# Weight sums of the first two Strassen chunks: GpSimd additions in SBUF instead of queue transfers and VectorE sums

## The chip, the cores and the metric

The kernel runs on one core of one Trainium2 chip. The metric is the device time of one launch in microseconds (us): lower is better, and the median of several runs counts. Five engines work side by side, each through its own list of instructions in order: TensorE (PE in the profile, with its weight loads shown apart as PEld), VectorE (DVE), ScalarE (ACT), GpSimd (POOL) and SyncE (SP). SP issues most transfers. POOL also has a transfer queue of its own, and only transfers of that queue are used here to add to what already lies in SBUF. About 0.2% of the time, 1.9 us, is what a measurement of this kernel can tell from no change.

## The reference: what is computed

The reference is a two-layer encoder trunk over 512 tokens of width 1024, in float32, with 256 memory tokens. Cut to its skeleton:

```
for i in range(2):
    h = rmsnorm(x, norm_g[i]);  mem_h = rmsnorm(mem, mem_norm_g[i])
    proj = h @ w_in                       # q, k, v of the mixer, q_mem, gate
    o_mix = mixer_dilated(...) if i == 0 else mixer_axial_gqa(...)
    o_mem = memory_attention(q_mem, mem_h, w_mem_kv[i], ...)
    y = concat(o_mix, o_mem) * silu(gate)
    x = x + y @ w_out[i]
```

Nearly all of the arithmetic is in the products with the weights `w_in`, `w_mem_kv` and `w_out`. Layer 0 has three groups of q, k and v of eight heads each, so its input projection is by far the widest. The value projection of the first group (columns 6144 to 7167 of `w_in_a`) and the memory queries (columns 9216 to 9727) are the two products that this change touches.

## The kernel before, in words

**Precision.** A float32 operand is split in a rounded high part and the low remainder, and a product is three matmuls: high by high (L178), low activation by high weight (L179), high activation by low weight (L182). For a weight tile of 128 by 1024 the high part `wh` is a cast by ScalarE (L333) and the low part `wo` is a subtraction by VectorE, `wo = wl - wh` (L347), with both inputs in SBUF. The first two chunks, the keys and values of the memory, have a variant with a gain (L331 and L345) and no Strassen sums.

**Strassen chunks.** All further weight products go in chunks (`s_chunk`), each by a Strassen-Winograd scheme of seven products. A chunk has four weight quarters, 11, 12, 21 and 22, and needs three more tiles that are sums of them, and the fourth of them in a quarter's place: T1 = 12 + 11, T2 = 22 + T1, T3 = 12 + 22, T4 = 21 + T2. The seven products take the weights in the order 21, 11, T1, T2, 22, T3, T4 (`ORDER`, L190). The activations' side has its own sums, made by VectorE from the transposed, normalized tokens: S1 and S3 straight from the transposes (L659, L660), S2 and S4 from those (L683, L685), each split in two parts by ScalarE and VectorE (L166 and L169, L671 and L674).

**The order of the chunks.** `PLAN` lists the chunks and `SEQ` their order: the memory keys and values (plan positions 1 and 2), then position 0, the value projection of the first head group, which is the first Strassen chunk, then position 3, the memory queries, which is the second, then the heads. In the code `c` is the plan position. Position 0 has two tiles to each quarter (below 21 of half 0 and of half 1, T1 of half 0, and so on); each of its fourteen steps is twelve matmuls of 128 by 512. Position 3 has one tile to a quarter, and seven steps.

**How the sums were made.** `Weights.dma` issues the loads from SP as far ahead as a limit on live tiles allows: for T1 the quarter 12 is loaded, for T2 the quarter 22. Then `Weights.sum`, called once per step, picks the first sum that is due:

- T1: VectorE adds tile 11 to it in SBUF (L291).
- T2: a transfer of POOL's queue adds tile T1 to it, SBUF to SBUF (L296).
- T3: a transfer of POOL's queue adds quarter 22 from memory (L301, issued in L260).
- T4: a transfer of POOL's queue adds tile T2 to tile 21, which is done with by then (L306).

"Due" is counted in steps, not in time: `self.g` counts steps, and a sum is due so many steps after its inputs were issued. For position 0 the first T1 is held until step 7 and the first T3 until step 10 (`SUM_AT`). So the place of a sum in its engine's list is fixed when the program is built, and the engine runs it when its semaphores allow. `hi` and `lo` (L319, L338) then make `wh` and `wo`, at most four tiles ahead of the matmuls (`RING`).

Of the kernel before, what the change touches and what calls it, by code (L numbers as in the profile page):

```python
# [13 lines left out]
ALU = mybir.AluOpType  # L14
# [27 lines left out]
SEQ = [1, 2, 0] + list(range(3, len(PLAN)))  # L42
T4_AT = {4: 4}
T1_DMA = 15
SUM_AT = {"T1": 7, "T3": 10}
KEEP_C = {0: 14, 3: 14, 4: 12}
KEEP = {"T2": 8, "T2b": 6, "W3": 10, "W1": 9, "W2": 10, "W2s": 9, "W1bs": 9, "W2c": 9, "W1b": 7, "W2b": 9, "W1o": 7}
# [86 lines left out]
def trunk_kernel(ctx: ExitStack, tc: tile.TileContext, x, mem, wall, norm_g, mem_norm_g, gcol,  # L134
                 qn_a, kn_a, qn_b, kn_b, ident_d, mask_d, tab_a, tab_b, out):
    nc = tc.nc
    V, A, G, T = nc.vector, nc.scalar, nc.gpsimd, nc.tensor
# [62 lines left out]
    class Weights:  # L200
        def __init__(self):
            self.items, self.last, self.need, self.allocs, self.sums = [], [], [], [], []
            self.users, self.kinds = {}, []
            g = 0
            for c in SEQ:
                kind, d = PLAN[c], sum(pieces(k) for k in PLAN[:c])
                base = len(self.items)
                if kind in GROUPS:
# [10 lines left out]
                else:  # L219
# [10 lines left out]
                    for k in order:  # L230
                        for x in range(n):
# [5 lines left out]
                            if k != "T4":  # L237
                                self.users[c, k, x] = 1 if k in ("22", "T3") or k == "11" and c >= T1_DMA else 2
                            g += 1
                self.kinds += [kind] * (g - len(self.kinds))  # L240
            assert sum(pieces(k) for k in PLAN) == wall.shape[0]
            self.g = -1
            self.live = 0
# [18 lines left out]
        def dma(self, most=9):  # L262
            while self.allocs and self.live < KEEP_C.get(self.allocs[0][0][0], KEEP[self.allocs[0][2]]) and most:
# [6 lines left out]
                    self.at[key] = self.g  # L270
                self.load(nc.sync, self.tile[key], d)

        def ripe(self, at, key, force, n=None):
            return key in at and (force or self.g - at[key] >= (LEAD if n is None else n))

        def sum(self, force=False, want=None):

            for n, (key, d) in enumerate(self.sums[:8]):
                if want and key != want:
                    continue  # L280
                c, k, x = key
                if not c and not force and self.g < SUM_AT.get(k, 0):
                    break
                if k == "T1" and c >= T1_DMA:
                    if not self.ripe(self.load_at, key, force):
                        continue
                    self.load(G, self.tile[key], d, accum_op=ALU.add)
                elif k == "T1":
                    if not (self.ripe(self.load_at, key, force, 4 if c in KEEP_C else None) and self.ripe(self.at, (c, "11", x), force)):
                        continue  # L290
                    V.tensor_tensor(self.tile[key], self.tile[key], self.tile[c, "11", x], ALU.add)  # L291
                    self.use((c, "11", x))
                elif k == "T2":
                    if not (self.ripe(self.load_at, key, force) and self.ripe(self.at, (c, "T1", x), force, 1 if c < T1_DMA else None)):
                        continue
                    G.dma_start(self.tile[key], self.tile[c, "T1", x], accum_op=ALU.add)  # L296
                    self.use((c, "T1", x))
                elif k == "T3":
                    if not self.ripe(self.load_at, key, force):
                        continue  # L300
                    self.load(G, self.tile[key], d, accum_op=ALU.add)  # L301
                else:
                    if not (self.ripe(self.lo_at, (c, "21", x), force, 1) and self.ripe(self.at, (c, "T2", x), force, T4_AT.get(c))):
                        continue
                    self.tile[key] = self.tile[c, "21", x]
                    G.dma_start(self.tile[key], self.tile[c, "T2", x], accum_op=ALU.add)  # L306
                    self.use((c, "T2", x))
                self.at[key] = self.g
                self.sums.pop(n)
                return True  # L310
            return False
# [7 lines left out]
        def hi(self, force=False):  # L319
            i = self.n_hi  # L320
            if i >= len(self.items) or not self.ripe(self.at, self.items[i], force, 1 if self.items[i][1] == "T1" and self.items[i][0] < T1_DMA else None):
                return False
# [1667 lines left out]
```

## Time and profile before

| | us |
|---|---|
| median of 3 runs (range) | 933.12 (932.94 to 933.17) |
| the profiled execution, its own time | 933.17 |
| its span, first to last instruction | 931.4 |
| TensorE busy | 924.8 |
| VectorE busy | 801.7 |
| ScalarE busy | 695.7 |
| GpSimd busy | 360.5 |

The profile is one execution on the chip. A row of the timeline gives the start in us from the span's start, the duration in us, the engine, the line of the kernel, the operation, the tile that it writes and those that it reads, the shape, and how many instructions are merged in the row (x2); in brackets stands the idle time of the engine just before it and what ended it. Spans of neighbours on one engine overlap a little, because each is reported with its start-up and its drain. A row with the engine PEld is a weight load of TensorE, which runs ahead of the matmul that uses it.

### The profile page before, as it was taken

The page shows a single profiled execution, that of the slowest core. Times are in us where ns is not written, and L with a number is a line of the kernel's source. Part 1 is how long each engine was busy: PE and PEld are TensorE (multiplying, and loading weights), DVE is VectorE, ACT ScalarE, POOL GpSimd, SP SyncE. Part 2 cuts the span into 40 slices and gives each one's busy share as a digit, 9 for nine tenths or more (in the row PEclk, how much of TensorE's full clock was granted, in tenths as well). Part 3 has the DMA queues.
Part 4 walks back from the last instruction along what each step waited for, and adds up shares of the span by engine and source line. Part 5 has one row for each costly group of instructions (what it writes and reads, how often), then busy time and mean ns, then how long its engine had stood idle before and what let it go on. Part 6 is the DMA issues. An engine that isn't in the chain of part 4 may idle for free.

```text
span 931.4 us, 16276 instructions
## 1 busy us (share of the span) xinstructions
PE 924.8 (99%) x5471; PEld 814.7 (87%) x5471; DVE 801.7 (86%) x1457; ACT 695.7 (75%) x1725; POOL 360.5 (39%) x504
## 2 busy tenths in 40 slices
PE   9999999999999999999999999999999999999998
PEld 7789888888888888888889998888988999999886
DVE  6999677879888888979798989999898998789977
ACT  7775789677868686867776767757879887789774
POOL 4411425556564646464746102234252440110122
PEclk9999999999999999999999999999999999999999
DMA  9999948968686778686867899999985687785777
GB/s 351 389 264 331 300 127 218 319 146 247 162 248 166 249 160 271 159 272 135 241 178 207 231 261 271 289 320 331 289 219 114 178 233 178 201 227 116 200 162 181
DMA packets 83179, 212.85 MB, mean 229 GB/s; under 512 B 18960, under 2 KB 25752, under 8 KB 83096
## 3 DMA queue, kind: packets, MB, share of 16 engines
q1 hardware_dynamic: 60744, 141.16, 42.3%
q0 software_dynamic: 20384, 67.12, 39.1%
q10 hardware_dynamic: 1968, 3.54, 1.0%
q8 instruction: 43, 0.70, 0.3%
q14 instruction: 40, 0.33, 0.1%
HBM read 162.96 MB, written 12.65 MB: 189 GB/s over the span
## 4 chain that ended last, share of the span: by engine, by line
PE 91%; DVE 5%; DMA 2%; ACT 1%; SPq 0%; issue 0%; DVEq 0%; ACTq 0%
PE pj L178 24%; PE pj L179 24%; PE pj L182 24%; PE qT L716 3%; PE sa L1476 2%; PE oo L1585 2%; PE ptb L1819 1%; PE sa L1472 1%; DVE wo L347 1%; PE pt L1564 1%; DMA x<-in_x_dram 1%; DMA row<-in_norm_g_dram 1%; PE ob L178 1%; PE ob L182 1%; PE ob L179 1%; PE xT L589 1%
## 5 line engine op out<-in xcount | busy, mean ns | idle before, releaser
L347 DVE TENSOR_TENSOR wo<-wl,wh 128x1024 fp32r<-128x1024 f32 x253 | 308.8, 1225 | 5.6 <-ACT wh L333 5.6
L333 ACT CAST wh<-wl 128x1024 fp32r<-128x1024 f32 x253 | 267.3, 1061 | 27.5 <-PE pj L179 19.5
L178 PE MATMUL pj<-wh,hS 128*128 128x512 f32 (+1 forms) x416 | 154.5, 380 | 0.0
L179 PE MATMUL pj<-wh,hS 128*128 128x512 f32 (+1 forms) x416 | 148.9, 367 | 0.0
L178 PE MATMUL pj<-wh,h 128*128 128x512 f32 (+1 forms) x312 | 115.3, 378 | 0.0
L179 PE MATMUL pj<-wh,h 128*128 128x512 f32 (+1 forms) x312 | 111.6, 367 | 0.0
L536 POOL TENSOR_TENSOR rstd<-mse,half 128x4 f32<-128x4 f32 (+2 forms) x98 | 102.0, 1041 | 8.2
L182 PE MATMUL pj<-wo,hS 128*128 128x512 f32 (+1 forms) x416 | 99.5, 366 | 0.0
L179 PEld LDWEIGHTS pj<-wh,hS 128*128 128x128 f32 x416 | 78.7, 189 | 11.2
L178 PEld LDWEIGHTS pj<-wh,hS 128*128 128x128 f32 x416 | 78.6, 189 | 11.0
L535 POOL TENSOR_SCALAR mse<-hss 128x4 f32<-128x4 f32 (+1 forms) x88 | 45.6, 519 | 104.4 <-ACT junk L704 91.3
L182 PEld LDWEIGHTS pj<-wo,hS 128*128 128x128 f32 x416 | 72.4, 189 | 13.0 <-DVE wo L347 0.2
L704 ACT ACTIVATE junk<-sn 128x128 f32<-128x128 f32 x264 | 79.3, 310 | 3.4 <-DVE sn L428 3.4
L260 POOL DMA_DIRECT2D wl<-in_wall_dram x44 | 41.9, 982 | 95.4 <-DMA wl<-in_wall_dram 21.7
L1417 POOL TENSOR_TENSOR ta<-sn,tabs 128x128 f32<-128x128 f32 (+1 forms) x64 | 38.3, 605 | 104.0 <-DVE sn L709 80.4
L415 ACT COPY sn<-pj 128x512 f32<-128x512 f32 x122 | 67.2, 590 | 12.3 <-PE pj L182 12.3
L182 PE MATMUL pj<-wo,h 128*128 128x512 f32 (+1 forms) x312 | 74.5, 366 | 0.0
L306 POOL DMA_DIRECT2D wl<-wl x35 | 31.0, 895 | 109.2 <-DVE wo L347 48.7
L438 DVE TENSOR_TENSOR sn<-pj,sn 128x512 f32<-128x512 f32 x89 | 60.7, 683 | 6.5 <-PE pj L182 6.2
L179 PEld LDWEIGHTS pj<-wh,h 128*128 128x128 f32 x312 | 59.0, 189 | 8.4
L178 PEld LDWEIGHTS pj<-wh,h 128*128 128x128 f32 x312 | 59.0, 189 | 8.2
L296 POOL DMA_DIRECT2D wl<-wl x35 | 32.9, 964 | 78.7 <-DVE wl L291 18.9
(299 smaller groups left out, 2403.0 us busy)
## 6 DMA issues: line engine op xcount, KB each, us to landing
wl<-in_wall_dram SPq DMA_DIRECT2D x226, 512.0 KB, 7.4
wl<-wl POOLq DMA_DIRECT2D x70, 512.0 KB, 5.9
wl<-in_wall_dram POOLq DMA_DIRECT2D x48, 512.0 KB, 8.6
od<-o SPq DMA_DIRECT2D x9, 256.0 KB, 5.8
x<-in_x_dram SPq DMA_DIRECT2D x4, 512.0 KB
v0r<-sn SPq DMA_DIRECT2D x8, 256.0 KB, 8.5
v0d<-v0r SPq DMA_DIRECT2D x4, 512.0 KB
og<-od ACTq DMA_DIRECT2D x4, 512.0 KB
```

The source lines that it names most:

```text
L178: T.matmul(o, a, b, start=start, stop=False, skip_group_check=True)
L179: T.matmul(o, c, d, start=False, stop=False, skip_group_check=True)
L182: T.matmul(o, a, b, start=False, stop=stop, skip_group_check=True)
L260: queue.dma_start(t, wall[d], **how)
L333: A.copy(wh, self.tile[key])
L347: V.tensor_tensor(wo, self.tile[key], wh.bitcast(F32), ALU.subtract)
L415: A.copy(t_, b_)
L438: V.tensor_tensor(t_, b_, t_, ALU.subtract if q == "12" and late is None else ALU.add)
L535: G.tensor_scalar(e, ss, EPS, None, ALU.add)
L536: G.tensor_tensor(r, e, half[:, 0:n], ALU.pow)
L704: A.activation(jk, p[:, j * 128:(j + 1) * 128], AF.Square, scale=by, accum_out=ss[:, j:j + 1])
L1417: G.tensor_tensor(ta[:, 0:n], xn[:, 0:n, 0:32], ropeA[:, 0, b, s0:s0 + n], ALU.mult)
```

## The change

`POOL_SUMS = 0, 3` names the plan positions 0 and 3, the first two Strassen chunks. For these, and only these, T1, T2 and T4 are additions by GpSimd on tiles in SBUF (`G.tensor_tensor`), each 128 by 1024 in float32 with both inputs in SBUF. For T1 this replaces VectorE's addition, for T2 and T4 the transfer of POOL's queue. T3 stays a transfer from memory. Position 0 has two tiles of each kind and position 3 one, so nine additions stand on GpSimd in place of three VectorE additions and six transfers. The steps at which the sums are due, and so the order in which they stand in the program, are the same.

```diff
+POOL_SUMS = 0, 3
...
+        def add(self, c, t, u):
+            if c in POOL_SUMS:
+                G.tensor_tensor(t, t, u, ALU.add)
+            else:
+                G.dma_start(t, u, accum_op=ALU.add)
+
...
                 elif k == "T1":
...
-                    V.tensor_tensor(self.tile[key], self.tile[key], self.tile[c, "11", x], ALU.add)
+                    (G if c in POOL_SUMS else V).tensor_tensor(self.tile[key], self.tile[key], self.tile[c, "11", x], ALU.add)
...
                 elif k == "T2":
...
-                    G.dma_start(self.tile[key], self.tile[c, "T1", x], accum_op=ALU.add)
+                    self.add(c, self.tile[key], self.tile[c, "T1", x])
...
-                    G.dma_start(self.tile[key], self.tile[c, "T2", x], accum_op=ALU.add)
+                    self.add(c, self.tile[key], self.tile[c, "T2", x])
```

## The prediction

> **What bounds the kernel now.** I read the page first, then TensorE's waits and busy time by stretch, then the engines' timelines from 30 to 75 us, where the nine sums lie, and last VectorE and GpSimd side by side around 200 us, where they meet.
>
> ```profile
> PE 924.8 (99%) x5471; PEld 814.7 (87%) x5471; DVE 801.7 (86%) x1457; ACT 695.7 (75%) x1725; POOL 360.5 (39%) x504
> PE 91%; DVE 5%; DMA 2%; ACT 1%; SPq 0%; issue 0%; DVEq 0%; ACTq 0%
> 30.00:40.00 10.00, 8.97 (x48) 7.38 (x47) 9.91 (x15) 8.34 (x13) 3.21 (x5) 1.00 1.03 409
> 50.00:60.00 10.00, 10.00 (x49) 8.12 (x48) 9.61 (x13) 8.13 (x13) 0.86 (x1) 1.00 1.07 227
> 200.00:300.00 100.00, 100.00 (x523) 84.86 (x522) 84.83 (x191) 75.39 (x229) 60.23 (x89) 1.00 0.73 198
> 920.00:932.00 12.00, 7.35 (x33) 5.76 (x31) 7.27 (x13) 0.39 (x1) 1.08 (x2) 0.95 0.72 219
> PE xT L589 <- DVE x L583: 1.0, 1, 1.0
> PEld pj L182 <- DVE wo L347: 0.2, 1, 0.2
> ```
>
> The third to sixth line are from the table by stretch (start, end, length, then busy us of PE, PEld, DVE, ACT and POOL, granted clock, transfer share, GB/s); the last two from the waits of TensorE and of its weight loads. TensorE is busy 924.8 of 931.4 us. Of the 6.6 us that it isn't, 1.0 us is the wait for `x` (at 31.6), some 4 us lie in the last 12 us, and the rest lies before 30 us. From `x` to the last stretch TensorE has no gap that shows as idle. So no sum that is ready earlier can buy more than that 1.0 us and the 0.24 us below; what makes TensorE wait in the middle costs its full length. The second thing to see is VectorE from 30 to 75 us: 9.91 and 9.61 of 10 us are busy. This stage has two full engines, and the change touches the second.
>
> **Which low parts are late.** Here is VectorE around the first chunk:
>
> ```profile
> 32.50 1.41 DVE L583 SCALAR_TENSOR_TENSOR x<-x,rstd,row 128x512 f32<-128x512 f32 x2
> 33.82 0.69 DVE L709 TENSOR_TENSOR xn<-pj,rstd 128x512 f32<-128x512 f32 x1
> 34.42 2.35 DVE L347 TENSOR_TENSOR wo<-wl,wh 128x1024 fp32r<-128x1024 f32 x2
> 36.69 0.69 DVE L709 TENSOR_TENSOR xn<-pj,rstd 128x512 f32<-128x512 f32 x1
> 37.29 1.22 DVE L291 TENSOR_TENSOR wl<-wl 128x1024 f32<-128x1024 f32 x1
> 38.42 0.69 DVE L659 TENSOR_TENSOR fS<-xT,f 128x512 f32<-128x512 f32 x1
> 39.02 0.68 DVE L660 TENSOR_TENSOR fS<-f,xT 128x512 f32<-128x512 f32 x1
> 39.80 0.69 DVE L169 TENSOR_TENSOR hS<-fS,hS 128x512 fp32r<-128x512 f32 x1
> 40.41 2.35 DVE L347 TENSOR_TENSOR wo<-wl,wh 128x1024 fp32r<-128x1024 f32 x2
> 42.68 1.22 DVE L291 TENSOR_TENSOR wl<-wl 128x1024 f32<-128x1024 f32 x1
> 43.81 0.68 DVE L659 TENSOR_TENSOR fS<-xT,f 128x512 f32<-128x512 f32 x1
> 44.41 0.68 DVE L660 TENSOR_TENSOR fS<-f,xT 128x512 f32<-128x512 f32 x1
> 45.18 0.69 DVE L169 TENSOR_TENSOR hS<-fS,hS 128x512 fp32r<-128x512 f32 x1
> 46.13 1.23 DVE L347 TENSOR_TENSOR wo<-wl,wh 128x1024 fp32r<-128x1024 f32 x1 [0.26 <-ACT wh L333]
> ...
> 53.52 1.22 DVE L347 TENSOR_TENSOR wo<-wl,wh 128x1024 fp32r<-128x1024 f32 x1
> 54.79 0.76 PEld L182 LDWEIGHTS pj<-wo,hS 128*128 128x128 f32 x4 [0.24 <-DVE wo L347]
> ```
>
> The low parts go in the order of the weights: the pair at 34.42 is quarter 21, that at 40.41 is 11, then T1 (half 0 at 46.13, half 1 in the rows left out) and T2 of half 0 at 53.52. It ends at 54.74, and the weight load that takes it starts at 54.79 after waiting 0.24 us. At this place TensorE has no slack towards VectorE: each us by which VectorE is later there is a us of the end.
>
> **Removed.** VectorE loses three additions, two of them before 53.52, and they take 1.13 us each from one start to the next (37.29 to 38.42): 2 x 1.13 = 2.3 us. Six transfers go. What did they cost? In ScalarE's timeline T2 of half 1 is waited for:
>
> ```profile
> 52.49 1.05 ACT L333 CAST wh<-wl 128x1024 fp32r<-128x1024 f32 x1 [0.75 <-DMA wl<-wl]
> ```
>
> That wait is ScalarE's, and TensorE shows none for it; I cost it at nothing gained.
>
> **Added: length of an addition.** No addition of 128 by 1024 by GpSimd stands in the trace. The nearest rows are the rope products of the heads, with two SBUF inputs, undisturbed:
>
> ```profile
> 199.21 0.32 POOL L1417 TENSOR_TENSOR ta<-sn,tabs 128x64 f32<-128x64 f32 x1 [3.88 <-DVE sn L709]
> 199.50 0.31 POOL L1418 TENSOR_TENSOR tb<-sn,tabs 128x64 f32<-128x64 f32 x1
> 226.44 0.47 POOL L1417 TENSOR_TENSOR ta<-sn,tabs 128x128 f32<-128x128 f32 x1 [1.76 <-DVE sn L709]
> 226.86 0.46 POOL L1418 TENSOR_TENSOR tb<-sn,tabs 128x128 f32<-128x128 f32 x1
> ```
>
> From start to start 64 elements take 0.29 us and 128 take 0.42: 2.03 ns for each more, which makes 0.42 + 896 x 2.03 ns = 2.24 us for 1024. By the durations (0.32 and 0.46) it is 2.42. I take 2.3, as an estimate with the ends 2.08 (1024 x 2.03 ns alone) and 2.42. The Trainium skill (GPSIMD Engine Reference, section 3.1) measured 4497 ns for an addition of 2048 elements; half of it, 2.25 us, is an estimate by that page, and the sum below would be 12.5 us by it.
>
> **Added: who is held up.** These rows stand in one stretch, VectorE and GpSimd:
>
> ```profile
> 223.13 1.54 POOL L1418 TENSOR_TENSOR tb<-sn,tabs 128x128 f32<-128x128 f32 x1
> 223.14 1.22 DVE L347 TENSOR_TENSOR wo<-wl,wh 128x1024 fp32r<-128x1024 f32 x1
> 224.28 1.48 DVE L291 TENSOR_TENSOR wl<-wl 128x1024 f32<-128x1024 f32 x1
> ```
>
> The same GpSimd product that takes 0.46 us alone takes 1.54: it stands still while VectorE's subtraction runs, to 224.36, and ends 0.31 us later. VectorE's next instruction, of two SBUF inputs too, takes 1.48 in place of 1.22: it is held while GpSimd reads. So the two exclude each other, in turns, and the one that waits goes next. With 128 elements a turn costs VectorE 0.26 us. Does it last for all of a long addition? No row shows it: between nothing (below nothing, no: an addition elsewhere can't speed VectorE up) and 2.3 us. The Trainium skill (SBUF — State Buffer, section "Who interferes with whom") says that a VectorE instruction with two SBUF inputs and a GpSimd instruction that reads SBUF block each other for the whole instruction; the trace agrees for 128 elements. I take the whole 2.3 us, because the rows show VectorE getting nothing until GpSimd is through. An instruction that reads PSUM (`xT`, `pj`) I let run beside it: L659, L660, L709, L438.
>
> **Added: when.** GpSimd is free in this stage, and its additions wait for nothing but loads and each other:
>
> ```profile
> 31.61 0.60 POOL L770 TENSOR_SCALAR rstd<-rstd,rm 128x4 f32<-128x4 f32 x2
> 44.77 2.11 POOL L260 DMA_DIRECT2D wl<-in_wall_dram  x2
> L260 SPq DMA_DIRECT2D wl<-in_wall_dram x5: 327/328/435, 16.1 to 20.0; - x5
> DMA to landing us min/median/max: 10.1/10.1/10.1
> L260 SPq DMA_DIRECT2D wl<-in_wall_dram x13: 327/328/328, 22.3 to 37.7; - x13
> ```
>
> The loads of this chunk begin at 16.1: the fifth, at 20.0, is for T1 of half 0 and lands at 30.1; the next ones, 1.28 us apart from 22.3, bring T1 of half 1 at 32.4, T2 by 35, and the second chunk's T1 and T2 (33.8 and 35.1) at 44 to 45.2. So the first addition starts when L770 ends, at 32.25. Played forward by turns, an estimate: T1 at 32.3, the first L583, T1 of half 1 at 35.2, the second L583, T2 at 38.2 under L709, a low part, T2 of half 1 at 41.6, a low part, the two issues of T3 (2.1 us by their row), T4 at 46.0, L169, T4 of half 1 at 48.9, a low part, and as nothing holds them back the second chunk's T1 at 52.4 and T2 at 55.8. All eight are through before T2's low part. What is queued behind them on GpSimd is the T3 transfers, issued as early as now, and nothing else.
>
> **The sum.** At T2's low part VectorE is later by 8 x 2.3 = 18.4 us, less the 2.3 us of its own sums, less what runs beside: 0.25 before L583 is up, 0.6 under L709, 0.8 and 1.2 under L659 and L660, together 2.9, less the 0.26 us of idle at 46.13. That is 18.4 - 2.3 - 2.9 - 0.3 = 12.9 us. TensorE takes all of it, as waits between 35 and 67 us. The ninth addition, T4 of the second chunk, comes under cover:
>
> ```profile
> 72.04 2.35 DVE L347 TENSOR_TENSOR wo<-wl,wh 128x1024 fp32r<-128x1024 f32 x2
> 77.24 1.12 PE L182 MATMUL pj<-wo,h 128*128 128x256 f32 x8
> ```
>
> The low part that ends at 73.2 is used at 77.24, 4 us of slack; I cost it at nothing, and 2.3 us if that cover were gone. After that TensorE is full and cannot make up. The profiled execution took 933.17 us and the median is 933.12, so one sum serves both: 933.2 + 12.9 = 946.1. With 2.08 or 2.42 us for an addition it is 944.3 or 947.1.
>
> **The rivals.** First, VectorE goes first: whenever it has a next instruction ready it keeps the turn, and additions get in only while it reads PSUM or idles. Then T1 at 32.25 costs 2.05 us, the one under L709 1.7, and three under pairs of PSUM readers (L659 with L660 twice, L438 once, taken as long) 1.1 each: 7.05 - 2.3 - 0.3 = 4.5, and 937.7 us. For it: such openings exist. Against it: L291 at 224.28 gave way to a product that had been waiting.
>
> Second, not slower: a long addition gives way to VectorE piece by piece, and the delay stays as small as in the rows of 128, 0.26 us. Eight of those are 2.1 us, and VectorE gets 2.3 back: no change, 933.1. It decides when the additions together cost VectorE less than 2.5 us before T2's low part. For it: no long addition was seen. Against it: in the rows, the held engine got nothing at all meanwhile.
>
> Third, faster by over 0.2%: it needs 1.9 us, and there are 1.0 and 0.24 us to have. The 1.0 us wait ends before any addition starts.
>
> Fourth, the change doesn't do what it says: a sum waits for an engine as before. Nothing of this is seen in the code, since T2 and T4 only change the engine.
>
> **How the numbers follow.** I give the forecast 0.60, VectorE-first and other partial holds (from 935 to 943) 0.23, no change 0.14, faster 0.03. Slower by over 0.2% (1.9 us, what can be told from no change) is 0.60 + 0.23 = 0.83. The forecast's own range is 944 to 947. I widen it upward to 949.5, where the ninth addition's cover fails too (947.1 + 2.3), and down to 936, which takes in the first rival and leaves out no change and faster, 0.17.
>
> **What would show it.** GpSimd rows of some 2.3 us with both tiles `wl`; L583 and L347 of VectorE between 32 and 58 us stretched to 3 us and more, L659 and L709 not; TensorE waits behind `x` of L583, `wo` of L347 and `hS`, near 13 us together before 70 us, and none new after; 64 SBUF-to-SBUF transfers of POOL's queue in place of 70. The prediction is wrong if VectorE's rows keep 1.22 us beside an addition, or if they stretch and TensorE doesn't wait.

## The result, and the profile after

| | before | after |
|---|---|---|
| median of 5 runs each on one chip (range), us | 933.17 (932.94 to 933.9) | 948.85 (947.84 to 949.49) |
| the profiled execution, us | 933.17 | 947.84 |
| its span, us | 931.4 | 945.8 |
| VectorE busy, us | 801.7 | 816.4 |
| GpSimd busy, us | 360.5 | 379.1 |

The change makes the kernel slower by 15.7 us: the time after is 1.0166 of the time before, with an interval of 1.0151 to 1.0181. The profiled executions differ by 14.7 us and their spans by 14.4, and it is these 14.4 us that the trace can account for.

The page of the kernel after: busy time of the engines, and the transfers of POOL's queue from SBUF to SBUF.

```profile
PE 928.4 (98%) x5471; PEld 816.5 (86%) x5471; DVE 816.4 (86%) x1454; ACT 695.9 (74%) x1725; POOL 379.1 (40%) x507
wl<-wl POOLq DMA_DIRECT2D x64, 512.0 KB, 5.6
```

VectorE has three instructions fewer (1454 for 1457) and is busy 14.7 us longer. GpSimd has three more (nine additions for six issues), and 64 transfers are left of 70. So the work moved as planned, and VectorE is busy for longer, not for less.

TensorE's waits after (what it waited for, us in total, times, the longest):

```profile
PE pj L183 <- DVE wo L354: 8.1, 1, 8.1
PE xT L596 <- DVE x L590: 3.0, 2, 2.7
```

Before there were 1.0 us for `x` and 0.2 for a weight load. (The lines moved by 1 or 7: L590 is the L583 of before, L354 is L347, L183 is L182, L170 is L169, L716 is L709, L666 is L659. L298 is T1's addition, L276 that of T2 and T4.) Now there is one wait of 8.1 us for a low part, and the waits for `x` are 2.0 us longer.

The table by stretch after (start, end, length, then busy us of PE, PEld, DVE, ACT and POOL, granted clock, transfer share, GB/s):

```profile
30.00:40.00 10.00, 7.02 (x37) 5.47 (x36) 10.00 (x8) 7.53 (x11) 9.92 (x8) 0.96 1.03 408
40.00:50.00 10.00, 8.10 (x30) 6.04 (x28) 9.90 (x6) 1.83 (x3) 10.00 (x6) 0.87 1.05 330
50.00:60.00 10.00, 3.79 (x10) 3.07 (x11) 9.65 (x7) 2.07 (x4) 5.82 (x4) 0.66 0.42 76
60.00:70.00 10.00, 10.00 (x48) 8.24 (x47) 9.93 (x14) 8.45 (x13) 0.00 (x0) 1.00 0.34 102
```

VectorE shows 9.65 to 10 of 10 us busy, as before. But from 30 to 60 us it finishes 21 instructions, where before it finished 40 (15, 12 and 13). Being held counts as busy. TensorE falls to 3.79 us in the third stretch, and its granted clock falls to 0.66; from 60 us on it is full again.

GpSimd's additions in the timeline after:

```profile
32.05 2.41 POOL L298 TENSOR_TENSOR wl<-wl 128x1024 f32<-128x1024 f32 x1
34.42 2.80 POOL L298 TENSOR_TENSOR wl<-wl 128x1024 f32<-128x1024 f32 x1
37.18 6.14 POOL L276 TENSOR_TENSOR wl<-wl 128x1024 f32<-128x1024 f32 x2
43.26 2.04 POOL L261 DMA_DIRECT2D wl<-in_wall_dram  x2
44.66 3.08 POOL L276 TENSOR_TENSOR wl<-wl 128x1024 f32<-128x1024 f32 x1
47.02 3.01 POOL L276 TENSOR_TENSOR wl<-wl 128x1024 f32<-128x1024 f32 x1
49.35 2.97 POOL L298 TENSOR_TENSOR wl<-wl 128x1024 f32<-128x1024 f32 x1
52.40 2.68 POOL L276 TENSOR_TENSOR wl<-wl 128x1024 f32<-128x1024 f32 x1
85.93 2.40 POOL L276 TENSOR_TENSOR wl<-wl 128x1024 f32<-128x1024 f32 x1 [30.04 <-issue]
```

Undisturbed, an addition takes 2.40 us (85.93). Eight of the nine lie between 32.05 and 55.08. The four at 32.05 to 37.18 come one after the other's end, with VectorE's instructions between them. The three at 44.66, 47.02 and 49.35 start 2.36 and 2.33 us apart while their rows are 3 us long, so each starts before the one ahead of it has ended.

VectorE in the same time, after:

```profile
32.38 2.63 DVE L590 SCALAR_TENSOR_TENSOR x<-x,rstd,row 128x512 f32<-128x512 f32 x1
34.93 2.84 DVE L590 SCALAR_TENSOR_TENSOR x<-x,rstd,row 128x512 f32<-128x512 f32 x1
37.69 0.68 DVE L716 TENSOR_TENSOR xn<-pj,rstd 128x512 f32<-128x512 f32 x1
38.29 2.79 DVE L354 TENSOR_TENSOR wo<-wl,wh 128x1024 fp32r<-128x1024 f32 x1
44.93 0.67 DVE L666 TENSOR_TENSOR fS<-xT,f 128x512 f32<-128x512 f32 x1
46.29 6.59 DVE L170 TENSOR_TENSOR hS<-fS,hS 128x512 fp32r<-128x512 f32 x1
52.80 3.35 DVE L354 TENSOR_TENSOR wo<-wl,wh 128x1024 fp32r<-128x1024 f32 x1
66.92 1.22 DVE L354 TENSOR_TENSOR wo<-wl,wh 128x1024 fp32r<-128x1024 f32 x1
86.08 3.34 DVE L354 TENSOR_TENSOR wo<-wl,wh 128x1024 fp32r<-128x1024 f32 x1 [0.30 <-ACT wh L340]
```

An instruction with two inputs in SBUF that meets an addition takes 2.6 to 3.4 us in place of 0.75 to 1.22; one that reads PSUM keeps its 0.67 or 0.68. The row to stay with is L170 at 46.29: 6.59 us instead of 0.69. It waited 5.9 us through three additions in a row, until 52.3. Only then comes quarter 11's low part of half 0 (52.80), which meets the eighth addition and ends at 56.15. The row at 66.92 is T2's low part of half 0, which started at 53.52 before: 13.4 us later.

The low-part matmuls of TensorE, before:

```profile
43.45 1.07 PE L182 MATMUL pj<-wo,h 128*128 128x512 f32 x4
46.17 1.07 PE L182 MATMUL pj<-wo,h 128*128 128x512 f32 x4
54.82 1.16 PE L182 MATMUL pj<-wo,hS 128*128 128x512 f32 x4
```

and after:

```profile
56.21 2.08 PE L183 MATMUL pj<-wo,h 128*128 128x512 f32 x4 [8.11 <-DVE wo L354]
60.64 1.08 PE L183 MATMUL pj<-wo,h 128*128 128x512 f32 x4
```

The first two are quarter 11, half 0 and half 1. Half 0 went from 43.45 to 56.21, 12.76 us later. Half 1 went from 46.17 to 60.64, 14.47 us later, and from there the shift stays: it is the span's 14.4 us. The step between the halves is 2.72 us before and 4.43 after. TensorE waited for nothing in those 1.7 us; it ran slow, and the four matmuls at 56.21 took 2.08 us for 1.07. The granted clock of some stretches of 2 us after (the column before the last two) shows why:

```profile
40.00:42.00 2.00, 2.00 (x6) 1.59 (x5) 2.00 (x2) 0.00 (x0) 2.00 (x1) 0.50 1.02 410
54.00:56.00 2.00, 0.00 (x0) 0.00 (x0) 2.00 (x1) 0.00 (x0) 1.90 (x2) 0.50 0.00 0
58.00:60.00 2.00, 2.00 (x7) 1.56 (x6) 1.65 (x3) 2.00 (x4) 0.00 (x0) 0.59 0.84 166
60.00:62.00 2.00, 2.00 (x10) 1.64 (x9) 1.97 (x3) 2.00 (x4) 0.00 (x0) 1.00 0.00 0
```

The granted clock was 0.50 at the end of the 8.1 us wait, 0.59 from 58 to 60 us and 1.00 from 60 us on: seven matmuls in 2 us, then ten. A mean of 0.59 over 2 us is half rate for some 1.6 of them, so half rate lasted from 56.2 to about 59.6 us, 3.4 us, and half of that is the 1.7 us. The Trainium skill (TensorE: Matmul & The Clock Gate, Part 1) says that TensorE runs at half rate after an idle window of about 3.4 us and gets its full rate back after as much work; this trace agrees as to these 3.4 us and the 8.1 us of waiting ahead of them. It does not agree that such a window is needed: the clock was 0.50 from 40 to 42 us too, behind a wait of only 2.7 us (for `x`, ending at 38.0). That time was lost ahead of the 8.1 us wait, which it only made shorter.

### The profile page after: what moved, and what is told of

It is laid out like the page before. It is cut to its first block, busy times and chain, and to the rows that moved or that the text cites. A ratio compares the mean times of both kernels' runs of the same rounds, so it can differ in the third digit from the quotient of the medians.

```text
span 945.8 us, 16279 instructions
## 1 busy us (share of the span) xinstructions
PE 928.4 (98%) x5471; PEld 816.5 (86%) x5471; DVE 816.4 (86%) x1454; ACT 695.9 (74%) x1725; POOL 379.1 (40%) x507
## 4 chain that ended last, share of the span: by engine, by line
PE 89%; DVE 6%; DMA 2%; issue 1%; ACT 1%; SPq 0%; DVEq 0%; ACTq 0%
PE pj L179 23%; PE pj L183 23%; PE pj L180 23%; PE qT L723 2%; DVE wo L354 2%; PE sa L1483 2%; PE oo L1592 2%; PE ptb L1826 1%; PE sa L1479 1%; PE pt L1571 1%; DMA x<-in_x_dram 1%; DMA row<-in_norm_g_dram 1%; PE ob L179 1%; PE ob L183 1%; PE ob L180 1%
## 5 line engine op out<-in xcount | busy, mean ns | idle before, releaser
L354 DVE TENSOR_TENSOR wo<-wl,wh 128x1024 fp32r<-128x1024 f32 x253 | 317.5, 1259 | 6.4 <-ACT wh L340 6.4
L278 POOL DMA_DIRECT2D wl<-wl x64 | 58.5, 938 | 151.7 <-DVE wo L354 48.3
L179 PE MATMUL pj<-wh,h 128*128 128x512 f32 (+1 forms) x312 | 116.7, 383 | 0.0
L180 PE MATMUL pj<-wh,h 128*128 128x512 f32 (+1 forms) x312 | 112.9, 371 | 0.0
L183 PE MATMUL pj<-wo,hS 128*128 128x512 f32 (+1 forms) x416 | 99.4, 365 | 0.0
L183 PE MATMUL pj<-wo,h 128*128 128x512 f32 (+1 forms) x312 | 75.7, 370 | 8.1 <-DVE wo L354 8.1
L183 PEld LDWEIGHTS pj<-wo,hS 128*128 128x128 f32 x416 | 72.5, 189 | 12.8
L422 ACT COPY sn<-pj 128x512 f32<-128x512 f32 x122 | 67.3, 590 | 12.3 <-PE pj L183 12.2
L261 POOL DMA_DIRECT2D wl<-in_wall_dram x44 | 41.6, 968 | 85.8 <-DMA wl<-in_wall_dram 26.4
L183 PEld LDWEIGHTS pj<-wo,h 128*128 128x128 f32 x312 | 55.1, 191 | 18.5 <-DVE wo L354 8.5
L445 DVE TENSOR_TENSOR sn<-pj,sn 128x512 f32<-128x512 f32 x89 | 60.8, 684 | 6.0 <-PE pj L183 5.7
```

The source lines that it names most:

```text
L179: T.matmul(o, a, b, start=start, stop=False, skip_group_check=True)
L180: T.matmul(o, c, d, start=False, stop=False, skip_group_check=True)
L183: T.matmul(o, a, b, start=False, stop=stop, skip_group_check=True)
L261: queue.dma_start(t, wall[d], **how)
L278: G.dma_start(t, u, accum_op=ALU.add)
L354: V.tensor_tensor(wo, self.tile[key], wh.bitcast(F32), ALU.subtract)
```

## The experiments

The theory is: each addition holds VectorE for its whole length wherever two-input SBUF work is queued, VectorE has no time to spare there, and TensorE pays at the first low part whose slack is used up. The rivals: GpSimd's mere activity in place of its reading; a wait of one particular tile; and, once the trace after was seen, the clock and the three additions in a row as costs of their own. The eleven kernels are all timed in 3 rounds beside the kernel before on the same chip (933.15 is from ten runs). "Against before" is the difference to the kernel before of the same call.

| experiment | median, us (range) | against before | ratio [interval] |
|---|---|---|---|
| e1_first: chunk 0 alone | 943.56 (943.01 to 944.0) | +10.0 | 1.0105 [1.0088, 1.0122] |
| e2_second: position 3 alone | 936.99 (936.33 to 937.63) | +3.5 | 1.0035 [1.0022, 1.0048] |
| e3_t1_only | 938.22 (937.85 to 938.36) | +4.7 | 1.0049 [1.0034, 1.0064] |
| e4_t2_t4 | 942.49 (941.67 to 942.87) | +9.0 | 1.0094 [1.0079, 1.0109] |
| e5_no_read: fills in place of additions | 933.15 (932.42 to 933.64) | -0.2 | 0.9994 [0.9985, 1.0003] |
| e6_fill: TensorE kept busy | 947.17 (946.86 to 948.1) | +13.8 | 1.015 [1.0135, 1.0165] |
| e7_t3_late | 945.5 (945.17 to 945.93) | +12.2 | 1.0131 [1.0116, 1.0146] |
| e8_later: the third Strassen chunk | 938.25 (936.36 to 938.36) | +4.9 | 1.0047 [1.003, 1.0064] |
| e9_halves | 946.6 (945.99 to 947.0) | +13.4 | 1.014 [1.0123, 1.0157] |
| e10_finish | 945.33 (945.01 to 946.26) | +12.0 | 1.0128 [1.0113, 1.0143] |
| e11_halves_finish | 944.53 (943.9 to 945.13) | +11.2 | 1.0118 [1.0101, 1.0135] |

**Is it the reading?** The kernel after with fills in the additions' places, which leaves the nine sums out:

```diff
-                G.tensor_tensor(t, t, u, ALU.add)
+                G.memset(t, 0.0)
...
-                    (G if c in POOL_SUMS else V).tensor_tensor(self.tile[key], self.tile[key], self.tile[c, "11", x], ALU.add)
+                    G.memset(self.tile[key], 0.0) if c in POOL_SUMS else V.tensor_tensor(self.tile[key], self.tile[key], self.tile[c, "11", x], ALU.add)
```

> The nine GpSimd additions are replaced by nine fills of the same tiles with zero, which read nothing; so the sums T1, T2 and T4 of the first two chunks are left out, and the places, the tiles written and the order are kept. Theory of turns (what holds VectorE is that GpSimd reads SBUF): no VectorE instruction is stretched, 932 to 934 us. Rival, GpSimd being busy or writing at all is what holds VectorE: the loss is in proportion to the fills' length, over 936 if they last more than 0.6 us each.

In the timeline of this kernel, GpSimd and VectorE:

```profile
40.71 2.39 POOL L276 MEMSET wl<- 128x1024 f32 x2
40.03 2.35 DVE L354 TENSOR_TENSOR wo<-wl,wh 128x1024 fp32r<-128x1024 f32 x2
```

Two fills run beside a pair of low parts, and the pair keeps its 2.35 us of before. The time is that of before (933.15). So GpSimd's writes and its place in the order cost nothing here: what costs is that an addition reads SBUF. A fill is shorter than an addition (some 1 us) and does not wait for the tile that an addition would read. But were it enough that GpSimd is busy, the pair would still have been stretched, and the rival put the time over 936 us for fills of more than 0.6 us. The Trainium skill (SBUF — State Buffer, "Who interferes with whom") says that a two-input VectorE instruction contends with a GpSimd instruction that reads SBUF and not with one that only writes; these rows agree. The kernel also answers what the change could have bought at best: with the three sums off VectorE and the six transfers gone, and nothing held up, there was no gain to measure.

**Which chunk?** `POOL_SUMS = 0,` and `POOL_SUMS = 3,`:

> Only the first chunk's six sums (T1, T2, T4 of both halves) are GpSimd additions; the second chunk's are as before. Theory of turns (a VectorE instruction with two SBUF inputs waits while GpSimd reads for an addition of 2.4 us, and TensorE pays at the low part with the least slack): 6 x 2.4 = 14.4, less 2.3 of VectorE's own sums, less about 2 that runs beside, is 10 us, and 0 to 1.7 us more if TensorE's granted clock falls after the wait again: 942 to 945 us. Theory of late sums (time is lost because sums reach TensorE's operands later through GpSimd's queue): the first chunk's sums are ready earlier than by transfer, so 933 to 935.

> Only the second chunk's three sums are GpSimd additions. Theory of turns: they stand behind the first chunk's transfers on GpSimd, which are issued until 52.9 us, so they run at 54 to 59 us; the low parts after 55 us have 1.4 to 2.9 us of slack, and VectorE saves one sum of 1.1 us: +1 to +3 us, 934 to 936. Theory that the time goes with the number of additions wherever they stand: a third of 15.7 us, 938. Theory of late sums: 933.

Six additions cost 10.0 us, as expected, three cost 3.5, a little above the bound. Together that is 13.5 and not 15.7. The second chunk's additions cost less when they come alone, since GpSimd then starts them later (the first at 53.56 us), when the low parts of the first chunk up to T1 are through. TensorE's timeline of `e2_second` shows where they are paid:

```profile
57.40 1.20 PE L183 MATMUL pj<-wo,hS 128*128 128x512 f32 x4 [2.51 <-DVE wo L354]
```

T2's low part of half 0 is the wait of 2.51 us: the very place, without slack, that the prediction named.

**Which sums?** T1 alone on GpSimd (T2 and T4 transfers again), and T2 and T4 alone (T1 on VectorE again):

```diff
# e3_t1_only
-            if c in POOL_SUMS:
-                G.tensor_tensor(t, t, u, ALU.add)
...
# e4_t2_t4
-                    (G if c in POOL_SUMS else V).tensor_tensor(self.tile[key], self.tile[key], self.tile[c, "11", x], ALU.add)
+                    V.tensor_tensor(self.tile[key], self.tile[key], self.tile[c, "11", x], ALU.add)
```

> Only the three T1 sums are GpSimd additions; T2 and T4 stay transfers of its queue. Theory of turns: three additions, 3 x 2.4 = 7.2, less 2.3 of VectorE's own and about 1 beside: +3 to +4 us, 936 to 937, if the third comes before T2's low part; +2 if it comes after. Theory of late sums: T1 is ready earlier and T2's transfer follows it: 933.

> T1 stays on VectorE, and T2 and T4 (six) are GpSimd additions. Theory of turns: VectorE keeps its own sums and spaces the additions out, since each T2 waits for a T1: four come before T2's low part, 4 x 2.4 = 9.6, less about 3.6 beside PSUM readers: +5 to +7 us, 938 to 940. Theory of late sums: T2 is ready 7 us earlier than by transfer: 933 or a little less.

Three additions of T1 cost 4.7 us although VectorE loses three of its own: more than expected. T2 and T4 cost 9.0, and here the expectation missed by over 2 us. GpSimd and VectorE in the timeline of `e4_t2_t4`:

```profile
48.62 5.30 POOL L276 TENSOR_TENSOR wl<-wl 128x1024 f32<-128x1024 f32 x2
47.75 7.25 DVE L354 TENSOR_TENSOR wo<-wl,wh 128x1024 fp32r<-128x1024 f32 x1
```

A low part of 1.22 us that began 0.9 us ahead of the two T4 behind T3's issue ended after both of them, 6 us late: it got no turn between them, though they start 2.3 us apart (48.62 and 50.94). Why the first one passed it, no row shows. But it is so in other runs too: low parts that began at 51.02 in `e7_t3_late`, 46.08 in `e10_finish` and 53.43 in `e2_second`, 0.1 to 0.5 us ahead of the first addition behind an issue, ended after that addition, with rows of 3.9 to 4.6 us. The alternation of the prediction fails at the same place as in the kernel after, so it is no accident of one run.

**Does the order of GpSimd make the long hold?** T3's two transfers issued behind the additions of T4 in place of ahead of them:

```diff
-SUM_AT = {"T1": 7, "T3": 10}
+SUM_AT = {"T1": 7, "T3": 13}
...
-                        break
+                        continue
```

> The kernel after, with the first chunk's two T3 transfers issued behind its T4 additions on GpSimd instead of ahead of them; nothing else moves. In the kernel after three additions ran in a row (T4, T4, and the second chunk's T1) while one VectorE instruction waited 5.9 us. If the transfers' issue just ahead is why no turn was given, turns alternate again here: no VectorE instruction waits more than 3 us, quarter 11's low part is done some 3 us earlier, and TensorE's wait for it is 5 us or less; the time is bounded by T2's low part, 0 to 2 us less than after. If not, the row of three stays and the time with it.

GpSimd and VectorE in the timeline of `e7_t3_late`:

```profile
37.74 12.28 POOL L276 TENSOR_TENSOR wl<-wl 128x1024 f32<-128x1024 f32 x4
46.87 0.92 DVE L170 TENSOR_TENSOR hS<-fS,hS 128x512 fp32r<-128x512 f32 x1
47.72 3.38 DVE L354 TENSOR_TENSOR wo<-wl,wh 128x1024 fp32r<-128x1024 f32 x1
```

Four additions in 12.28 us are 3.07 each, so VectorE gets in between them; L170 takes 0.92 us in place of 6.59. The time falls by 3.3 us against the kernel after, more than expected. The longest wait of VectorE is now 3.3 us (the low part at 51.02, 4.48 us long), for one addition. So the order of GpSimd's list did make the long hold. Behind the issue there now stand only the second chunk's T1 and T2, and T2 reads what T1 wrote, so these two cannot overlap: the run does not tell the issue from the additions that can overlap behind it.

**Is it what runs behind the issue that overlaps?** In `e10_finish` an operation on one column of the tile follows each addition of T2 and T4; it needs the sum, so it waits until the addition has ended.

```diff
                 G.tensor_tensor(t, t, u, ALU.add)
+                G.tensor_scalar(t[:, 0:1], t[:, 0:1], 0.0, None, ALU.add)
```

> The kernel after, with a one-column GpSimd instruction behind each T2 and T4 addition that adds zero to the first column of what the addition wrote; it has to wait for the addition's end, so the next addition can't begin before. Nothing is left out. In the kernel after, three additions that followed the T3 transfers' issue overlapped (starts 2.36 us apart, rows of 3.0) and one VectorE instruction waited for all three. If that overlap is what denies VectorE its turn, no VectorE instruction waits for more than one addition here, and the time falls to that of the kernel with T3 late or below: 944 to 946.5 us. If VectorE simply loses its turn there for another reason, the wait of 5.9 us stays: 948.5 to 950.

GpSimd, VectorE and TensorE in its timeline:

```profile
46.54 3.04 POOL L276 TENSOR_TENSOR wl<-wl 128x1024 f32<-128x1024 f32 x1
50.72 2.36 POOL L276 TENSOR_TENSOR wl<-wl 128x1024 f32<-128x1024 f32 x1
44.94 5.73 DVE L355 TENSOR_TENSOR wo<-wl,wh 128x1024 fp32r<-128x1024 f32 x2
51.95 1.68 DVE L170 TENSOR_TENSOR hS<-fS,hS 128x512 fp32r<-128x512 f32 x1
66.41 1.20 PE L183 MATMUL pj<-wo,hS 128*128 128x512 f32 x4 [0.15 <-DVE wo L355]
```

The two T4 now start 4.18 us apart, with a turn of VectorE between them: a pair of low parts takes 5.73 us, 3.4 more than its 2.35, and L170 waits 1 us. The time falls by 3.5 us, as expected. So VectorE gets its turn back where each addition has to end before the next one begins. An operation of one column that does not read the sum was not run, so the forced end and the mere presence of another instruction are not told apart. The last row is T2's low part of half 0 on TensorE: used at 54.82 before, it comes 11.6 us later and TensorE waits for it.

**Shorter holds.** Each addition, T1's too, as two of 512 columns (`e9_halves`, without the line `G.tensor_scalar`), and the same with the operation on one column behind each half (`e11_halves_finish`, with it):

```diff
-                G.tensor_tensor(t, t, u, ALU.add)
+                for h in (slice(0, 512), slice(512, 1024)):
+                    G.tensor_tensor(t[:, h], t[:, h], u[:, h], ALU.add)
+                    G.tensor_scalar(t[:, h.start:h.start + 1], t[:, h.start:h.start + 1], 0.0, None, ALU.add)
...
-                    (G if c in POOL_SUMS else V).tensor_tensor(self.tile[key], self.tile[key], self.tile[c, "11", x], ALU.add)
+                    if c in POOL_SUMS:
+                        self.add(c, self.tile[key], self.tile[c, "11", x])
+                    else:
...
```

> The kernel after, with each of the nine additions as two of 512 columns, one behind the other; nothing is left out. If a turn is one GpSimd instruction, VectorE gets in twice as often: its instructions between 32 and 58 us wait 1.3 us at a time instead of 2.4 or more, GpSimd's work is spread over more of VectorE's, and part of it falls behind the low parts without slack: 940 to 946 us. If GpSimd keeps the turn as long as it has work queued, the rows of VectorE stay stretched by 2.4 us and more and the time stays at 948 to 950.

> The kernel with each addition in halves of 512 columns, with the same one-column instruction behind each half. In the kernel with halves alone, VectorE's instructions waited 1.3 us at a time until the T3 transfers' issue, and then one waited 9.3 us for seven halves. If overlap denies the turn, no wait here is over 1.5 us, GpSimd's work is spread over more of VectorE's instructions, part of it falls behind the low parts without slack: 939 to 945 us. If not, a wait of 7 us or more stays and the time is 946 or over.

GpSimd and VectorE in the timeline of `e9_halves`:

```profile
31.88 14.32 POOL L277 TENSOR_TENSOR wl<-wl 128x512 f32<-128x512 f32 x8
47.55 10.46 POOL L277 TENSOR_TENSOR wl<-wl 128x512 f32<-128x512 f32 x8
48.57 10.00 DVE L170 TENSOR_TENSOR hS<-fS,hS 128x512 fp32r<-128x512 f32 x1
```

The first eight halves took 14.32 us, with VectorE's work between them. The eight behind T3's issue took 10.46, one overlapping the next, and L170 got nothing for 9.3 us: the rest of one half and some seven more, at 1.31 us each. It is the same hold as in the kernel after, made longer. The time of 946.6 us lies between the two ranges that were expected. With the forced ends (`e11_halves_finish`) the longest hold of VectorE is 1.7 us (`f`, 2.36 us for 0.69, at 53.71), a little over the 1.5 expected, and the time is 944.53. So short, strict turns are worth some 4.3 us of the 15.7; 11.2 us against the kernel before stay.

**What is the clock worth?** The kernel after, with thirty matmuls of a tile of zeros, added to the product's bank without changing it, ahead of the late low part of quarter 11:

```diff
+FILL = [30]
...
+                if i == 1 and FILL:
+                    for _ in range(FILL.pop()):
+                        T.matmul(bank[s][0][:, 0:128], zero, zero, start=False, stop=False, skip_group_check=True)
```

> The kernel after, with 30 matmuls of zeros added in TensorE's list just ahead of the low matmuls of quarter 11, half 0, where it waited 8.1 us; they add zero to the sum, and nothing is left out. If 1.7 us of the loss is the lower granted clock behind that wait, TensorE leaves the wait at full clock: 1 to 1.7 us less than the kernel after, and the granted clock from 56 to 60 us is 1.0. Rival, the slow matmuls there are VectorE's or a transfer's doing: no change, and the clock falls again.

TensorE's rows in its timeline:

```profile
56.27 1.21 PE L184 MATMUL pj<-wo,h 128*128 128x512 f32 x4 [1.47 <-DVE wo L355]
59.16 1.07 PE L184 MATMUL pj<-wo,h 128*128 128x512 f32 x4
68.25 0.76 PEld L184 LDWEIGHTS pj<-wo,hS 128*128 128x128 f32 x4 [0.54 <-DVE wo L355]
```

and the stretch that answers to the one with the clock of 0.59:

```profile
58.00:60.00 2.00, 2.00 (x10) 1.50 (x8) 1.65 (x3) 2.00 (x4) 0.00 (x0) 1.00 0.84 166
```

At full clock the halves lie 2.89 us apart instead of 4.43, and 1.5 us are won there. But then T2's low part of half 0, used at 54.79 before, makes TensorE wait again, 0.54 us at 68.25, which is 13.46 us later than before. So the lost clock costs the difference, 14.47 - 13.46 = 1.0 us by the traces. By the medians it is 1.7 us, and the intervals of the two ratios overlap, so the time alone does not settle it. The rows do for these two profiled executions.

**The same change elsewhere.** `POOL_SUMS = 4,`, the third Strassen chunk, whose additions ran between 77 and 104 us, where VectorE had been busy 7.87, 4.98 and 8.37 of 10 us in the three stretches from 80 us on:

> The first two chunks are as before; in their place the third Strassen chunk's (head 0's) six sums are GpSimd additions, at 95 to 150 us, where VectorE is busy three quarters of the time. Theory of turns: each addition still stretches VectorE by up to 2.4 us, but the low parts have slack there, so TensorE loses little: 933 to 936. Theory that an addition costs 1.5 us or so wherever it stands: 6 x 1.5 = 9, 942.

The expectation was too low: 4.9 us for six additions. TensorE did not wait for a low part here. Rows of GpSimd, VectorE and TensorE:

```profile
99.21 5.17 POOL L276 TENSOR_TENSOR wl<-wl 128x1024 f32<-128x1024 f32 x2
99.26 2.89 DVE L716 TENSOR_TENSOR sn<-sn,rstd 128x512 f32<-128x512 f32 x1 [1.25 <-POOL rstd L543]
102.07 2.86 DVE L435 TENSOR_TENSOR sn<-sn 128x512 f32<-128x512 f32 x1
105.78 0.50 PE L179 MATMUL pj<-wh,h 128*128 128x512 f32 x1 [2.00 <-DVE sn L445]
```

Two instructions of VectorE were held for an addition each (L716 and L435), and behind them in VectorE's list stood L445, which empties the PSUM bank that the next product needed. The low parts have slack there, but what stands behind the held instruction did not. Behind TensorE's wait of 2.0 us its granted clock fell again, to 0.60 from 106 to 108 us and 0.54 from 108 to 110. By these figures half rate lasted some 3.4 us and cost 1.7 us (an estimate). With the wait of 2.0 us and another of 0.6 for L716 that is 4.3 of the 4.9 us.

## Why the prediction was right, and where its steps failed

- **Nothing to gain: right.** `e5_no_read` keeps every benefit of the change without the reading and takes the time of before.
- **Full turns, VectorE held: right.** L590, L170 and L354 are held for whole additions and L716 and L666 are not. The rows are 2.6 to 3.4 us long, where the prediction looked for 3 and more. The second rival (0.26 us for each, 933.1) falls by the row at 32.38, 2.63 us in place of 0.75. The first (VectorE goes first, 937.7) allows that row, since that addition began before VectorE asked. It falls by the row at 34.93: the second L590 was next in VectorE's list, and the addition queued at 34.42 still got the turn before it. An addition has 2.40 us against the 2.3 taken, inside the ends 2.08 to 2.42. By the Trainium skill (GPSIMD Engine Reference, section 3.1) the estimate was 2.25.
- **VectorE's delay at T2's low part: right in size, in part by luck.** Forecast 12.9 us, found 13.4 (53.52 to 66.92). The eight additions at 2.4 in place of 2.3 are 0.8 us more, so the difference is of the size that the addition's length gives. But the forecast counted on strict turns, and the kernel did not keep them. Where they are kept, in `e10_finish`, the same low part starts at 65.14, 11.6 us late. By the same sum with 2.4 us, some 5 us of the additions then run beside other work, where the forecast took 2.9 (an estimate). The long hold made up for what the forecast left out.
- **"The one that waits goes next": failed for three of the eight.** It holds for the first four additions. Behind T3's issue the two T4 and the second chunk's T1 ran without a gap, and L170 waited 5.9 us. `e4_t2_t4`, `e9_halves`, `e7_t3_late` and `e10_finish` show that this comes from additions that overlap one another, that it goes with the issue ahead of them, and that it is undone when each must end first. It costs VectorE 1.8 us at T2's low part (66.92 against 65.14), and it moved the delay forward.
- **Where TensorE pays: failed.** The prediction found no slack at T2's low part and so let TensorE pay 12.9 us there. It paid 12.76 us four steps earlier, at quarter 11's low part. That one ended near 41.6 before (the first of the pair at 40.41) and was used at 43.45, with 1.8 us to spare; after it ended at 56.15, 14.5 us later, and 14.5 - 1.8 = 12.7. Waits came as one of 8.1 and two of 3.0 together, 11 us, in place of near 13; the rest is slow matmuls. The long hold moved the place: in `e10_finish`, with strict turns, TensorE's last wait in this stage is at T2's low part, 11.6 us late there, and the kernel is 12.0 us slower. That is the place that the prediction named.
- **A term that the sum lacked: the clock.** One long wait lowers it, and 3.4 us at half rate cost 1.7 us. Of these 0.7 would have been lost at T2's low part anyway, as `e6_fill` shows, so 1.0 us is its price. The 1.0 us is what is left of 14.47 beside 13.46, so that the two add up is no test of them.
- **What was costed at nothing: right.** The ninth addition stretches the low part at 86.08 to 3.34 us and TensorE has no wait there.
- **One sum for the profiled execution and the median: off by 1 us.** The two agreed before. After, the median of 948.85 lies 1.0 us above the profiled execution, which is the shortest of the five. The mean granted clock of the other four was 0.992 to 0.994 against 0.995, so a part may be the clock; they have no trace, and it is not shown.

**What stays open.** Why additions overlap behind the issue and not ahead of it is not known. The Trainium skill (GPSIMD Engine Reference, section 2.1) warns that consecutive GpSimd instructions are no barrier between its cores, which would fit, but no row here shows single cores. How long an idle time lowers the clock is not settled either: waits of 3.7 us and more did, and of those between 2.0 and 2.7 us some did and some did not.

## What to carry to other kernels

An idle engine is no free place for a sum when its reads shut out the engine that is full: count the busy time of VectorE's two-input instructions in that stage first, and take a GpSimd addition there as up to its whole length lost by VectorE. In the six kernels that place whole additions of this size on GpSimd by chunk or by kind, three to nine of them, each cost the kernel 0.8 to 1.7 us. Then ask what stands behind the held instruction in its engine's list, low parts and the emptying of banks alike, and try the fill variant first: if the time does not move when the operation costs nothing, no placement of it can pay.

## What the runs showed of the hardware that was not expected

- The hold of VectorE by GpSimd is not bounded by one instruction. Additions in a row that overlap kept one VectorE instruction of 0.69 us waiting for 5.9 us, and more than seven half additions kept one for 9.3. A dependent operation of one column behind each addition of T2 and T4 ends that and makes the kernel 3.5 us faster (948.85 to 945.33), though it is more work.
- Splitting the additions alone gains only 2.2 us (946.6 us), and the halves behind the issue still overlap; halves that must end take 944.53 us.
- A wait of TensorE costs more than its length when it is long: behind 8.1 us of waiting, matmuls took twice their time for 3.4 us. Shorter waits did it in some runs: 2.7 us in the kernel after, 2.0 in `e8_later`.
